# An encoder layer on one core: products queued behind the first score of their attention unit, and new places for the second half's buffers

## The chip, the cores and the metric

The kernel runs on one core of one Trainium2 chip. The metric is device microseconds of one execution, told as the median of several runs. The engines are named as the profile names them: PE (TensorE matmuls), PEld (its weight loads), DVE (VectorE), ACT (ScalarE), POOL (GpSimd) and SP (the queue from which nearly all DMAs are issued). SBUF is the on-chip memory, PSUM holds the results of matmuls, DRAM is the chip's large memory.

## What is computed

One layer of an encoder: windowed attention with grouped heads, then a SwiGLU feed-forward net (FFN), each between two norms and with shift, scale and gate from a modulation vector. Sequence 2048, width 1024, 16 query heads on 4 key heads of 64, FFN width 2816, all in float32. The reference, cut to what matters:

```python
mod = (c_act @ ada_w[i] + ada_b[i])[:, None, :]
sh1, sc1, g1, sh2, sc2, g2 = jnp.split(mod, 6, axis=-1)
h = rmsnorm(x, mix_norm_pre[i]) * (1.0 + sc1) + sh1
y = windowed_gqa_sink(h, att_w_qkv[j], att_w_o[j], att_sink[j], rel_bias)
x = x + g1 * rmsnorm(y, mix_norm_post[i])
h = rmsnorm(x, ffn_norm_pre[i]) * (1.0 + sc2) + sh2
y = swiglu(h, ffn_w_in[i], ffn_w_out[i])
x = x + g2 * rmsnorm(y, ffn_norm_post[i])
```

In `windowed_gqa_sink` every block of 128 queries sees three blocks of 128 keys, with a bias by distance and one more "sink" logit in the softmax.

## The kernel before

**Products.** Each float32 operand is split into a high part (ACT, L151) and the rest (DVE or POOL, L152), and a product of two 128-row blocks is three matmuls (`three`, L146 to L148). The tokens stand in four chunks of 512 columns. A "product" below means one such matmul of 512 columns.

**Stages.** First the queries, keys and values of chunks 0 and 1, and the first modulation rows (L238 to L366). Then attention: 64 units (`Unit`, L408), one for each block of 128 queries and key head. `scores` makes, for each of four heads, two score matmuls (L430), a DVE operation that adds the bias and finds the maximum (L435), and an exponential on ACT (L437); then POOL scales the rows by the reciprocal sum (L443). `values` runs LAG = 2 units later: three times four transposes on PE (L453), a split, and two value products (L458, L459); DVE puts the result together (L466). The scores have two PSUM banks (`psS`).

**Fillers.** While a unit waits for DVE, ACT and POOL, PE has other products to do. They come from generators: in the first 32 units the queries, keys and values of chunks 2 and 3 (`fillers_qkv`, L469: 24 tiles of 24 products), in the last 32 the output projections of chunks 0 to 2 (`fillers_o`, L593: again 24 tiles of 24). `Budget.pull` (L608) takes them out after each unit, 19 products per unit in the first half and 20 in the second (`FILL`, L47). The last six tiles of chunk 2 (`HOLD`, L54) are held until the last unit's first score. What is left after the last unit is drained (L667).

**What orders the work.** The program order is only a priority. A planner simulates the program's engines and queues and fixes, for each engine, the order of its instructions: at each moment the earliest instruction in program order that is ready by its reckoning. On the chip each engine then keeps that order and waits by semaphores. `tc.issue_after(ins)` adds an order: what is written inside on the engine of `ins` comes behind `ins` in that engine's queue. Each tile pool is a fixed stretch of SBUF from the left or the right; a tile of a new pool that lies over an old one waits until the old tiles there are no longer used. Tiles with the same tag share that tag's buffers.

**Around the projections.** `OProj.fill` (L521) loads the attention output (`ol`, four buffers), splits it, and makes eight tiles per chunk, each with its weight (`wo`). For chunk 0 the weight comes raw from `w_o` (one raw buffer), is split with POOL and stored in split form; chunks 1 and 2 load the split form (three buffers). After each tile it advances `ends` of the chunk before (L570): the norm's statistics, eight residuals (L502; three POOL operations each), statistics again, eight `make_h2` (L497), which store the FFN's input `h2_d`. Chunk 3 (`last_o`, L679) runs by itself after attention, and the ends of chunks 2 and 3 run as `late_residuals` (L837) beside the first FFN half, one step per block.

**Modulation rows.** `ada_load` and `ada_reduce` (L254, L259) make one of 48 rows of 128 numbers from a 512 KB weight and one DVE operation. Rows 0 to 24 are made before attention, rows 25 to 39 in units 1 to 31, two units between load and reduction, in the two raw buffers of the pool `ws`, which the fillers' raw weights share; rows 40 to 47 in units 34 to 50 (`ADA_UNITS`, L52).

**The FFN.** It uses a seven-product scheme for two by two blocks (`Block`, L739): each block of weights has four DVE sums, and each half of the sequence needs seven operands, some of them differences of `h2_d` blocks (`differences`, L701). For the first half these are made at the start: `h_blocks` (L877) loads blocks, two differences on DVE make the first two operands (L887, L888), then the blocks are loaded again for the rest. For the second half the differences are made within `late_residuals` and stored in `hd_d`, from which `Operands.load` (L731) gets them.

Of the kernel before, what the change touches and what calls it, by code (L numbers as in the profile page):

```python
# [11 lines left out]
F32 = mybir.dt.float32  # L12
# [33 lines left out]

FILL = (19, 20)  # L47
LAG = 2


ADA_A = 9
ADA_UNITS = (range(1, 32, 2), range(34, 52, 2))  # L52

# [18 lines left out]
def encoder_layer(ctx, tc, a):  # L72
# [4 lines left out]
    def open_pool(stack, name, bufs=1, side="left", space=None):  # L77
# [15 lines left out]
            for j in range(HT // 2)] for i in range(S // HALF)]  # L93
    hd_d = [{n: dram.tile([P, CH], F32, name=f"hd_d{j}_{n}") for n in OPERANDS if n[0] == "t"} for j in range(KT // 2)]
    h2_d = [dram.tile([P, KT, CH], F32, name=f"h2_d{c}") for c in range(NCH)]
# [142 lines left out]
    with ExitStack() as pa:  # L238
# [11 lines left out]
        sp.dma_start(cb_d, cb)  # L250
        cbs = [cb]
        tc.keep_in_program_order(act.preload_act_table_set("natural_log_exp_and_others"))
# [6 lines left out]
        def ada_reduce(t, w):  # L259
            dve.tensor_tensor_reduce(w, w, cbs[-1], 1.0, adab[:, t:t + 1], ALU.mult, ALU.add, mod[:, t:t + 1])  # L260

# [240 lines left out]
    def residual(c, k, y, xr, r, acc, alloc, eng=dve):  # L502
# [7 lines left out]
        else:  # L510
            sq = alloc(f"xsq{c}_{k}")
            act.activation(sq, y, AF.Square)
            pool.tensor_tensor(acc, acc, sq, ALU.add)

    class OProj:

# [4 lines left out]
        def fill(self, prev=None, hold=None):  # L521
# [11 lines left out]
            for n in range(KT):  # L533
                w = wop.tile([P, 2, KT, P], F32R, tag="w", name=f"wo{c}_{n}", bufs=2 if c == NCH - 1 else 3)
                if c in (0, NCH - 1):
                    raw = wop.tile([P, KT, P], F32, tag="raw", name=f"wor{c}_{n}", bufs=3 if c else 1)
                    sp.dma_start(raw, a["w_o"][n])
                    split(w[:, 0], w[:, 1], raw, dve if c else pool)
                    if c == 0:
                        sp.dma_start(wo_d[n], f(w))  # L540
                else:
                    sp.dma_start(f(w), wo_d[n])
                ps = psF.tile([P, CH], F32, tag="mm", name=f"py{c}_{n}")
                for k in range(KT):
# [77 lines left out]


    ada_units = [*ADA_UNITS[0], *ADA_UNITS[1]]
    HALF_ADA = len(ADA_UNITS[0]) - 1
    late = list(range(2 * KT + ADA_A, 6 * KT))
    units = [Unit(c, g, jb) for c in range(NCH) for g in range(KVH) for jb in range(JB)]
# [4 lines left out]
    oend = ExitStack()  # L632
    op = wop = yp = None
    for i, un in enumerate(units):
        if i == half:
            assert not waiting
# [17 lines left out]
        if i == 0:  # L654
            waiting = []
        if i in ada_units:
            for w in waiting:
                with tc.issue_after(un.red):
                    ada_reduce(*w)
            waiting = [ada_load(late.pop(0), ws if i < half else yp)] if i != ada_units[HALF_ADA] and late else []  # L660
# [7 lines left out]
    assert not late and not waiting  # L668
    dve.tensor_tensor(coef[:, 3, :], mod[:, 40:48], gains[:, 3, :], ALU.mult)
    att.close()  # L670
# [24 lines left out]
    def temp(name, tag="t", bufs=None):  # L695
        return tmp.tile([P, CH], F32, tag=tag, name=name, bufs=bufs)

    def temp0(name):
        return tmp0.tile([P, CH], F32, tag="t", name=name)

    def differences(b11, b12, b21, b22, give, engs=(pool, dve)):  # L701

        give("b11", b11)
        give("b21", b21)
        engs[0].tensor_tensor(b11, b12, b11, ALU.subtract)
        engs[1].tensor_tensor(b12, b22, b12, ALU.subtract)
        give("t3", b12)
        give("t1", b11)
        give("b22", b22)
        engs[0].tensor_tensor(b22, b22, b11, ALU.subtract)  # L710
        give("t2", b22)
        engs[1].tensor_tensor(b21, b21, b22, ALU.subtract)
        give("t4", b21)

    class Operands:
# [6 lines left out]
        def slot(self, n, k):  # L722
# [3 lines left out]
            return self.ops[n][k]  # L726

        def put(self, n, k, src):
            split(*self.slot(n, k), src, dve)

# [106 lines left out]
    def late_residuals():  # L837

        for c in range(CPH, NCH):
# [15 lines left out]
            for k in range(0, KT, 2):  # L855
# [6 lines left out]
                if c == NCH - 1:  # L862
                    first = [temp(f"ld{k + e}") for e in range(2)]
                    for e in range(2):
                        sp.dma_start(first[e], h2_d[c - 1][:, k + e, :])
                    differences(first[0], hs_[0], first[1], hs_[1],
                                lambda n, t: sp.dma_start(hd_d[k // 2][n], t) if n[0] == "t" else None)
                yield

    late = late_residuals()  # L870
    b21p = open_pool(early, "b21", K2)
    t3p = open_pool(early, "t3", K2)
    st0 = ExitStack()
    tmp0 = open_pool(st0, "tmp0", 10)
    half = Operands("0", K2, None)

    def h_blocks(k, names, st):  # L877
        b = []
        for n in names:
            b.append(temp0(f"fx{k}_{n}_{st}"))  # L880
            sp.dma_start(b[-1], h2_d[int(n[2]) - 1][:, 2 * k + (n[1] == "2"), :])
        return b

    with tc.high_priority(offset=1):
        for k in range(K2):
            b11, t1, t2 = h_blocks(k, ("b11", "b12", "b22"), 0)
            dve.tensor_tensor(t1, t1, b11, ALU.subtract)  # L887
            dve.tensor_tensor(t2, t2, t1, ALU.subtract)  # L888
# [9 lines left out]
    st0.close()  # L898
    tmp = open_pool(ffn, "tmp", 10, side="right")
    for hf in range(S // HALF):  # L900
        for t in range(HT - 2 if hf + 1 < S // HALF else HT - 1):
            hid = Hidden(half, t, hf)
            for i in range(7):
                hid.step(i)
            if hf == 0:
                next(late, None)
        if hf + 1 < S // HALF:
            pair = [Hidden(half, t, hf) for t in range(HT - 2, HT)]
            half = Operands("1", K2, lambda n, k: hd_d[k][n] if n[0] == "t" else
                            h2_d[CPH + int(n[2]) - 1][:, 2 * k + (n[1] == "2"), :])  # L910
            interleaved(pair, half)
    hid = Hidden(half, HT - 1, hf)
    for i in range(5):
# [231 lines left out]
```

## Time and profile before

| | us |
|---|---|
| median of 3 runs | 2191.41 |
| lowest to highest | 2188.45 to 2195.57 |
| the profiled execution | 2197.15 |
| its span in the trace | 2195.3 |
| first score of unit 0 | 181.3 |
| last product of the first half | 450.6 |
| first product of the projections | 482.2 |
| first score of unit 63, the last | 734.7 |

All times in the trace are microseconds from the span's start. A line of the timeline has the start, the duration, the engine (SPq: SP's queue), the line of the program, the operation, what it writes and reads, and in brackets the idle time before it with what ended it. A row of the stages has the stretch, its length, for each engine the busy time and the number of instructions, the clock that PE was granted (1.00 is full speed), the busy share of the DMA engines and GB/s; a row that is asked for a single line shows that line's instructions alone. Matmul records overlap, so the distance between two starts, not the duration, is what a matmul costs. A few records are missing from the trace.

### The profile page before, as it was taken

The page shows a single profiled execution, that of the slowest core. Times are in us where ns is not written, and L with a number is a line of the kernel's source. Part 1 is how long each engine was busy: PE and PEld are TensorE (multiplying, and loading weights), DVE is VectorE, ACT ScalarE, POOL GpSimd, SP SyncE. Part 2 cuts the span into 40 slices and gives each one's busy share as a digit, 9 for nine tenths or more (in the row PEclk, how much of TensorE's full clock was granted, in tenths as well). Part 3 has the DMA queues.
Part 4 walks back from the last instruction along what each step waited for, and adds up shares of the span by engine and source line. Part 5 has one row for each costly group of instructions (what it writes and reads, how often), then busy time and mean ns, then how long its engine had stood idle before and what let it go on. Part 6 is the DMA issues. An engine that isn't in the chain of part 4 may idle for free. (4 is left out here: it accounts for less than half of the span.)

```text
span 2195.3 us, 28935 instructions
## 1 busy us (share of the span) xinstructions
PE 2072.1 (94%) x9366; PEld 1677.9 (76%) x9366; DVE 1668.4 (76%) x2917; ACT 1080.6 (49%) x2125; POOL 774.2 (35%) x695
## 2 busy tenths in 40 slices
PE   6998999989989998899999989999999999998997
PEld 4786878767777776778888868888888788877886
DVE  8657676676766579877888797766664788999987
ACT  4546565677757664443434353333332654465432
POOL 3403333355696865434344522222221000220040
PEclk8998999999999999999999999999999999999998
DMA  8786665576865683444445663223231544348442
GB/s 287 252 272 225 189 195 166 167 232 213 301 222 204 202 311 129 152 163 153 161 156 180 220 226 110 107 101 115 101 105 41 205 149 148 127 152 278 158 130 101
DMA packets 195764, 390.05 MB, mean 178 GB/s; under 512 B 19563, under 2 KB 61596, under 8 KB 190492
## 3 DMA queue, kind: packets, MB, share of 16 engines
q1 hardware_dynamic: 195036, 387.68, 53.0%
q8 instruction: 74, 1.21, 0.2%
q14 instruction: 78, 0.64, 0.1%
q10 hardware_dynamic: 576, 0.52, 0.1%
HBM read 268.55 MB, written 119.57 MB: 177 GB/s over the span
## 5 line engine op out<-in xcount | busy, mean ns | idle before, releaser
L435 DVE CUSTOM_DVE_ANT_0 pr<-s,bias,nsink 128x384 f32<-128x384 f32 (+1 forms) x256 | 149.1, 595 | 121.6 <-PE s L430 100.0
L147 PE MATMUL pc_i<-ht,ws_i 128*128 128x512 f32 x528 | 207.2, 392 | 1.0 <-DVE ht L152 1.0
L146 PE MATMUL pc_i<-ht,ws_i 128*128 128x512 f32 x528 | 207.5, 393 | 0.6 <-DVE u_i L813 0.6
L148 PE MATMUL pc_i<-ht,ws_i 128*128 128x512 f32 x528 | 207.0, 392 | 0.0
L823 POOL TENSOR_TENSOR p_i<-p_i,u_i 128x512 f32<-128x512 f32 x44 | 80.0, 1818 | 326.8 <-DVE u_i L810 180.9
L437 ACT ACTIVATE pr<-pr,nm 128x385 f32<-128x385 f32 (+1 forms) x256 | 154.0, 605 | 72.3 <-DVE nm L435 64.2
L958 POOL TENSOR_TENSOR z<-z,z 128x512 f32<-128x512 f32 x32 | 53.8, 1696 | 358.6 <-DVE z L954 338.4
L443 POOL TENSOR_SCALAR pr<-pr,rs 128x384 f32<-128x384 f32 (+1 forms) x256 | 146.3, 591 | 92.4 <-DVE rs L441 90.5
L430 PE MATMUL s<-k,q 128*128 128x384 f32 (+1 forms) x512 | 138.9, 368 | 23.4 <-DVE nm L435 15.7
L151 ACT CAST ws_i<-s_i 128x512 fp32r<-128x512 f32 x132 | 81.5, 619 | 128.4 <-PE pc_i L148 122.3
L146 PE MATMUL pc_i<-hb,wa_i 128*128 128x512 f32 x352 | 139.3, 396 | 0.6 <-DVE b_i L807 0.6
L151 ACT CAST wa_i<-wiri 128x512 fp32r<-128x512 f32 x132 | 81.9, 620 | 117.2 <-PE pc_i L148 111.1
L148 PE MATMUL pc_i<-hb,wa_i 128*128 128x512 f32 x352 | 138.9, 395 | 0.0
L147 PE MATMUL pc_i<-hb,wa_i 128*128 128x512 f32 x352 | 138.8, 394 | 0.0
L152 DVE TENSOR_TENSOR plo<-t,phi 128x512 fp32r<-128x512 f32 x184 | 121.7, 683 | 13.2 <-ACT phi L151 12.3
L430 PEld LDWEIGHTS s<-k,q 128*128 128x128 f32 x512 | 89.7, 200 | 46.8 <-DVE nm L435 29.9
L146 PEld LDWEIGHTS pc_i<-ht,ws_i 128*128 128x128 f32 x528 | 99.3, 188 | 24.4 <-issue 1.0
L147 PEld LDWEIGHTS pc_i<-ht,ws_i 128*128 128x128 f32 x528 | 99.2, 188 | 23.7 <-DVE ht L152 1.5
L453 PE MATMUL t<-ident,pr 128*128 128x128 f32 x736 | 114.0, 281 | 2.5 <-DVE plo L152 2.3
L148 PEld LDWEIGHTS pc_i<-ht,ws_i 128*128 128x128 f32 x528 | 99.2, 188 | 22.2
L152 DVE TENSOR_TENSOR ws_i<-s_i,ws_i 128x512 fp32r<-128x512 f32 x132 | 107.7, 816 | 5.0 <-ACT ws_i L151 4.7
L152 DVE TENSOR_TENSOR wa_i<-wiri,wa_i 128x512 fp32r<-128x512 f32 x132 | 106.1, 804 | 5.6 <-ACT wa_i L151 5.3
(323 smaller groups left out, 6200.3 us busy)
## 6 DMA issues: line engine op xcount, KB each, us to landing
wiri<-w_in SPq DMA_DIRECT2D x88, 512.0 KB, 4.7
ada<-ada_w SPq DMA_DIRECT2D x48, 512.0 KB, 5.5
wiro<-w_out SPq DMA_DIRECT2D x48, 384.0 KB, 3.8
q_d<-e SPq DMA_DIRECT2D x64, 256.0 KB, 4.1
q<-q_d SPq DMA_DIRECT2D x16, 1024.0 KB, 5.5
wo<-wo_d SPq DMA_DIRECT2D x16, 1024.0 KB, 6.0
g_d_b<-p_i SPq DMA_DIRECT2D x44, 256.0 KB, 4.8
g_d_t<-p_i SPq DMA_DIRECT2D x40, 256.0 KB, 2.0
```

Of the source, the lines that this page charges most:

```text
L146: pe.matmul(ps, w[0], h[0], start=first, stop=False)
L147: pe.matmul(ps, w[0], h[1], start=False, stop=False)
L148: pe.matmul(ps, w[1], h[0], start=False, stop=last)
L151: act.copy(hi, src)
L152: return eng.tensor_tensor(lo, src, f(hi), ALU.subtract).ins
L430: m = pe.matmul(ps[:, :n], q[:, h, jb * P:(jb + 1) * P], kk[:, i, (jb + j0) * P:(jb + j1) * P], start=i == 0, stop=i == 1)
L435: red = dve.tensor_tensor_reduce(pr[:, h, :n], ps[:, :n], bias[g][:, h, j0 * P:j1 * P], -1.0, nsink[:, hh:hh + 1], ALU.add, ALU.min, nm[:, ...
L437: act.activation(pr[:, h, :n + 1], pr[:, h, :n + 1], AF.Exp, bias=nm[:, h:h + 1], scale=-1.0, accum_out=rs[:, h:h + 1])
L443: pool.tensor_scalar(pr[:, h, :n], pr[:, h, :n], rs[:, h:h + 1], 1.0, ALU.mult, ALU.mult)
L453: pe.transpose(pt[:, h * P:(h + 1) * P], pr[:, h, jj * P:(jj + 1) * P], ident)
L823: pool.tensor_tensor(sa, sa, b, ALU.mult)
L958: (pool if (i, x) in ((2, 2), (4, 4), (5, 5), (6, 6)) else dve).tensor_tensor(sums[hf, n2, x], sums[hf, n2, x], sums[hf, n2, y], ALU.add)
```

## The change

- **Products.** `FILL` becomes (18, 14), and `fill.pull` runs inside `tc.issue_after(un.first)`: on PE, whatever a pull writes stands behind the first score matmul of its unit. The final drain is outside.
- **Places.** The pools of the first half stand in another order (xs and nrm lowest, then hs and ev). The weight pool `ws` moves to the attention's own pools on the right and stays for both halves; the projection's weights use it too (`wop = ws`), with two buffers, and two raw ones for chunk 0. The pool of the o tiles, now six buffers, is opened lowest, where xs lay; 12 y buffers in place of 14. At the FFN's start `wi0` lies below `hA`.
- **Modulation.** Only rows up to 39 are made during attention. Rows 40 to 47 are made in the FFN (`late_ada`), each in two halves of 512 columns, one step per block after the late residuals; the second copy of the vector in the second half of attention is gone, and `coef[:, 3]` is made there.
- **The first FFN half's operands.** `OProj.ends` of chunk 1 makes the differences after each two `make_h2`, both engines' share on DVE, and stores the t operands in `hd_d[0]`; the FFN's start loads all operands from DRAM with `half.load`. `h_blocks`, `temp0` and `put` go. `ends` yields eight times in other places: after every fourth residual and every second `make_h2`.

```diff
-FILL = (19, 20)
+FILL = (18, 14)
...
-ADA_UNITS = (range(1, 32, 2), range(34, 52, 2))
+ADA_UNITS = range(1, 32, 2)
+
+OBUFS = 6
...
     com = ExitStack()
+    xs = open_pool(com, "xs", 8)
+    nrm = open_pool(com, "nrm")
     hs = open_pool(com, "hs", 2 * KT)
     ev = open_pool(com, "ev", 2)
-    nrm = open_pool(com, "nrm")
-    xs = open_pool(com, "xs", 8)
...
-    ws = open_pool(com, "ws", 2)
+    wop = ws = open_pool(att, "ws", 2, side="right")
...
-                t = op.tile([P, 2, 2, CH], F32R, tag="o", name=f"ol{c}_{g}", bufs=4)
+                t = op.tile([P, 2, 2, CH], F32R, tag="o", name=f"ol{c}_{g}", bufs=4 if c == NCH - 1 else OBUFS)
...
-                w = wop.tile([P, 2, KT, P], F32R, tag="w", name=f"wo{c}_{n}", bufs=2 if c == NCH - 1 else 3)
+                w = wop.tile([P, 2, KT, P], F32R, tag="w", name=f"wo{c}_{n}", bufs=2)
                 if c in (0, NCH - 1):
-                    raw = wop.tile([P, KT, P], F32, tag="raw", name=f"wor{c}_{n}", bufs=3 if c else 1)
+                    raw = wop.tile([P, KT, P], F32, tag="raw", name=f"wor{c}_{n}", bufs=3 if c else 2)
...
-                y = yp.tile([P, CH], F32, tag="y", name=f"y{c}_{n}", bufs=4 if c == NCH - 1 else 14)
+                y = yp.tile([P, CH], F32, tag="y", name=f"y{c}_{n}", bufs=4 if c == NCH - 1 else 12)
...
-                if k % 3 == 2:
+                if k % 4 == 3:
                     yield
-            yield
             r = self.stats("x", c)
             yield
             for k in range(KT):
                 make_h2(self.ys[k], c, k, r)
-                if k % 3 == 2:
+                if k % 2:
+                    if c == CPH - 1:
+                        first = [yp.tile([P, CH], F32, tag="xr", name=f"hf{j}", bufs=3) for j in (k - 1, k)]
+                        for j in range(2):
+                            sp.dma_start(first[j], h2_d[c - 1][:, k - 1 + j, :])
+                        differences(first[0], self.ys[k - 1], first[1], self.ys[k],
+                                    lambda n, t: sp.dma_start(hd_d[0][k // 2][n], t) if n[0] == "t" else None, (dve, dve))
                     yield
...
-    late = list(range(2 * KT + ADA_A, 6 * KT))
+    late = list(range(2 * KT + ADA_A, 5 * KT))
...
             com.close()
+            op = open_pool(oend, "op", OBUFS)
             yp = open_pool(oend, "yp")
-            cb = yp.tile([P, D], F32, tag="cb", name="cb2")
-            sp.dma_start(cb, cb_d)
-            cbs.append(cb)
-            wop = open_pool(oend, "wop", 2)
-            op = open_pool(oend, "op", 4)
             fill = Budget(fillers_o())
...
-        fill.pull(FILL[i >= half])
+
+        with tc.issue_after(un.first):
+            fill.pull(FILL[i >= half])
...
-    dve.tensor_tensor(coef[:, 3, :], mod[:, 40:48], gains[:, 3, :], ALU.mult)
     att.close()
...
+    wi = [open_pool(early, "wi0"), None]
     hA = open_pool(early, "hA", KT // 2)
-    wi = [open_pool(early, "wi0"), None]
...
+    def late_ada():
+
+        for i in range(2):
+            cols = slice(i * CH, (i + 1) * CH)
+            cb = temp(f"cb{i}", "r", 2)
+            sp.dma_start(cb, cb_d[:, cols])
+            for t in range(5 * KT, 6 * KT):
+                w = temp(f"ada{t}_{i}", "r", 2)
+                sp.dma_start(w, a["ada_w"][t][:, cols])
+                yield
+                dve.tensor_tensor_reduce(w, w, cb, 1.0, (mod if i else adab)[:, t:t + 1], ALU.mult, ALU.add, mod[:, t:t + 1])
+        dve.tensor_tensor(coef[:, 3, :], mod[:, 40:48], gains[:, 3, :], ALU.mult)
+
+    late = chain(late_residuals(), late_ada())
...
-    half = Operands("0", K2, None)
+    half = Operands("0", K2, lambda n, k: hd_d[0][k][n] if n[0] == "t" else
+                    h2_d[int(n[2]) - 1][:, 2 * k + (n[1] == "2"), :])
     with tc.high_priority(offset=1):
-        for k in range(K2):
-            b11, t1, t2 = h_blocks(k, ("b11", "b12", "b22"), 0)
-            dve.tensor_tensor(t1, t1, b11, ALU.subtract)
-            dve.tensor_tensor(t2, t2, t1, ALU.subtract)
-            half.put("b11", k, b11)
-            half.put("t2", k, t2)
+        half.load("b11", "t2")
...
     with tc.high_priority(offset=100):
-        for k in range(K2):
-            differences(*h_blocks(k, ("b11", "b12", "b21", "b22"), 1),
-                        lambda n, t: half.put(n, k, t) if n not in ("b11", "t2") else None)
+        half.load(*[n for n in OPERANDS if n not in ("b11", "t2")])
...
-            if hf == 0:
-                next(late, None)
+            next(late, None)
```

More of the change, by code (lines that the diff above doesn't have):

```diff
@@ L93, in encoder_layer @@
             for j in range(HT // 2)] for i in range(S // HALF)]
-    hd_d = [{n: dram.tile([P, CH], F32, name=f"hd_d{j}_{n}") for n in OPERANDS if n[0] == "t"} for j in range(KT // 2)]
+    hd_d = [[{n: dram.tile([P, CH], F32, name=f"hd_d{i}_{j}_{n}") for n in OPERANDS if n[0] == "t"}
+             for j in range(KT // 2)] for i in range(S // HALF)]
     h2_d = [dram.tile([P, KT, CH], F32, name=f"h2_d{c}") for c in range(NCH)]
@@ L250, in encoder_layer @@
         sp.dma_start(cb_d, cb)
-        cbs = [cb]
         tc.keep_in_program_order(act.preload_act_table_set("natural_log_exp_and_others"))
@@ L259, in ada_reduce @@
         def ada_reduce(t, w):
-            dve.tensor_tensor_reduce(w, w, cbs[-1], 1.0, adab[:, t:t + 1], ALU.mult, ALU.add, mod[:, t:t + 1])
+            dve.tensor_tensor_reduce(w, w, cb, 1.0, adab[:, t:t + 1], ALU.mult, ALU.add, mod[:, t:t + 1])
         wres = {}
@@ L513, in residual, with differences @@
             pool.tensor_tensor(acc, acc, sq, ALU.add)
+    def differences(b11, b12, b21, b22, give, engs=(pool, dve)):
+        give("b11", b11)
+        give("b21", b21)
+        engs[0].tensor_tensor(b11, b12, b11, ALU.subtract)
+        engs[1].tensor_tensor(b12, b22, b12, ALU.subtract)
+        give("t3", b12)
+        give("t1", b11)
+        give("b22", b22)
+        engs[0].tensor_tensor(b22, b22, b11, ALU.subtract)
+        give("t2", b22)
+        engs[1].tensor_tensor(b21, b21, b22, ALU.subtract)
+        give("t4", b21)
     class OProj:
@@ L621, in drain @@
             self.pull(1e9)
-    ada_units = [*ADA_UNITS[0], *ADA_UNITS[1]]
-    HALF_ADA = len(ADA_UNITS[0]) - 1
-    late = list(range(2 * KT + ADA_A, 6 * KT))
+    late = list(range(2 * KT + ADA_A, 5 * KT))
     units = [Unit(c, g, jb) for c in range(NCH) for g in range(KVH) for jb in range(JB)]
@@ L632, in encoder_layer @@
     oend = ExitStack()
-    op = wop = yp = None
+    op = yp = None
     for i, un in enumerate(units):
         if i == half:
-            assert not waiting
+            assert not waiting and not late
             fill.drain()
@@ L655, in encoder_layer @@
             waiting = []
-        if i in ada_units:
+        if i in ADA_UNITS:
             for w in waiting:
@@ L659, in encoder_layer @@
                     ada_reduce(*w)
-            waiting = [ada_load(late.pop(0), ws if i < half else yp)] if i != ada_units[HALF_ADA] and late else []
+            waiting = [ada_load(late.pop(0), ws)] if late else []
         if i >= LAG:
@@ L667, in encoder_layer @@
     fill.drain()
-    assert not late and not waiting
-    dve.tensor_tensor(coef[:, 3, :], mod[:, 40:48], gains[:, 3, :], ALU.mult)
     att.close()
@@ L696, in temp @@
         return tmp.tile([P, CH], F32, tag=tag, name=name, bufs=bufs)
[L698 to L713, printed above, removed]
     class Operands:
@@ L726, in slot @@
             return self.ops[n][k]
-        def put(self, n, k, src):
-            split(*self.slot(n, k), src, dve)
         def load(self, *names):
@@ L866, in late_residuals @@
                     differences(first[0], hs_[0], first[1], hs_[1],
-                                lambda n, t: sp.dma_start(hd_d[k // 2][n], t) if n[0] == "t" else None)
+                                lambda n, t: sp.dma_start(hd_d[1][k // 2][n], t) if n[0] == "t" else None)
                 yield
-    late = late_residuals()
+    def late_ada():
[10 more added lines that the diff above has]
+    late = chain(late_residuals(), late_ada())
     b21p = open_pool(early, "b21", K2)
     t3p = open_pool(early, "t3", K2)
-    st0 = ExitStack()
-    tmp0 = open_pool(st0, "tmp0", 10)
-    half = Operands("0", K2, None)
[L877 to L882, printed above, removed]
-    with tc.high_priority(offset=1):
-        for k in range(K2):
-            b11, t1, t2 = h_blocks(k, ("b11", "b12", "b22"), 0)
-            dve.tensor_tensor(t1, t1, b11, ALU.subtract)
-            dve.tensor_tensor(t2, t2, t1, ALU.subtract)
-            half.put("b11", k, b11)
-            half.put("t2", k, t2)
+    half = Operands("0", K2, lambda n, k: hd_d[0][k][n] if n[0] == "t" else
+                    h2_d[int(n[2]) - 1][:, 2 * k + (n[1] == "2"), :])
+    with tc.high_priority(offset=1):
+        half.load("b11", "t2")
     lasto.close()
@@ L894, in encoder_layer @@
     with tc.high_priority(offset=100):
-        for k in range(K2):
-            differences(*h_blocks(k, ("b11", "b12", "b21", "b22"), 1),
-                        lambda n, t: half.put(n, k, t) if n not in ("b11", "t2") else None)
-    st0.close()
+        half.load(*[n for n in OPERANDS if n not in ("b11", "t2")])
     tmp = open_pool(ffn, "tmp", 10, side="right")
@@ L904, in encoder_layer @@
                 hid.step(i)
-            if hf == 0:
-                next(late, None)
+            next(late, None)
         if hf + 1 < S // HALF:
             pair = [Hidden(half, t, hf) for t in range(HT - 2, HT)]
-            half = Operands("1", K2, lambda n, k: hd_d[k][n] if n[0] == "t" else
+            half = Operands("1", K2, lambda n, k: hd_d[1][k][n] if n[0] == "t" else
                             h2_d[CPH + int(n[2]) - 1][:, 2 * k + (n[1] == "2"), :])
             interleaved(pair, half)
+    assert next(late, None) is None
     hid = Hidden(half, HT - 1, hf)
```

## The prediction

> **What bounds the kernel now.** First the page's busy times:
>
> ```profile
> span 2195.3 us, 28935 instructions
> PE 2072.1 (94%) x9366; PEld 1677.9 (76%) x9366; DVE 1668.4 (76%) x2917; ACT 1080.6 (49%) x2125; POOL 774.2 (35%) x695
> ```
>
> TensorE (PE) is the bound, but its 94% is the busy share of pipelined records and hides slow stretches. So next the busy times by stage. I cut at the first score (181), the end of the first half of attention (461), the last unit's first score (735), the end of projection chunk 2 (786), the end of chunk 3 (840) and the first FFN blocks (900); the last row is a quiet FFN stretch.
>
> ```profile
> core 0: us, PE busy (x) PEld busy (x) DVE busy (x) ACT busy (x) POOL busy (x), PEclk, DMA share, GB/s
> 241.00:461.00 220.00, 212.62 (x1099) 175.09 (x1097) 149.49 (x386) 135.21 (x326) 80.63 (x126) 1.00 0.61 184
> 461.00:735.00 274.00, 249.21 (x1218) 199.00 (x1219) 188.47 (x466) 193.19 (x439) 197.58 (x228) 0.96 0.66 230
> 735.00:786.00 51.00, 46.90 (x220) 37.72 (x219) 27.10 (x45) 33.89 (x70) 38.34 (x38) 0.97 0.76 237
> 786.00:840.00 54.00, 51.84 (x226) 42.20 (x226) 45.90 (x52) 36.00 (x59) 36.86 (x15) 1.00 0.76 273
> 840.00:900.00 60.00, 47.26 (x183) 36.31 (x182) 54.68 (x75) 27.78 (x44) 28.13 (x13) 0.91 0.39 136
> 1330.00:1700.00 370.00, 370.00 (x1611) 302.02 (x1610) 244.18 (x353) 111.86 (x186) 84.32 (x56) 1.00 0.27 96
> ```
>
> The last row prices a product: 370 / 1611 = 0.230 us for 512 columns. By that price chunk 3 (226 x 0.230 = 52.0 of 54 us) is nearly full, and the FFN's start (183 x 0.230 = 42.0 of 60) loses 18 us. For attention I need the other matmuls, from the timeline on PE, by the distance from one start to the next:
>
> ```profile
> 219.03 0.85 PE L430 MATMUL s<-k,q 128*128 128x384 f32 x4
> 219.72 0.40 PE L147 MATMUL psq<-lo,ws 128*128 128x512 f32 x1
> ...
> 231.74 0.60 PE L453 MATMUL t<-ident,pr 128*128 128x128 f32 x4
> 232.09 0.60 PE L430 MATMUL s<-k,q 128*128 128x384 f32 x2
> ```
>
> Four scores take 0.69 us (0.172 each), four transposes 0.35 (0.087 each). A unit's own work is 8 scores, 12 transposes and 6 value products: 1.38 + 1.05 + 1.38 = 3.8 us. Then the counts by line and stage, products (L146 is every third one) first, scores second:
>
> ```profile
> 241.00:461.00 220.00, 61.50 (x153) 28.58 (x152) 1.00 0.61 184
> 461.00:735.00 274.00, 57.66 (x144) 27.23 (x145) 0.96 0.66 230
> ...
> 241.00:461.00 220.00, 51.19 (x198) 33.46 (x198) 1.00 0.61 184
> 461.00:735.00 274.00, 69.49 (x252) 43.67 (x252) 0.96 0.66 230
> ```
>
> First half: 459 products (105.6 us) and 198 / 8 = 24.75 units (94.1) fill 200 of 220 us; **20 us lost**. Second half: 432 products (99.4) and 31.5 units (119.7) fill 219 of 274; **55 us lost**. Those two and the FFN's start (18) are what a rearrangement can win.
>
> Why they are lost shows at single places. In the first half the raw weight slots are shared with the modulation rows:
>
> ```profile
> 303.60 0.34 SPq L256 DMA_DIRECT2D ada<-ada_w  x1
> 316.20 0.39 SPq L482 DMA_DIRECT2D wsr<-w_qkv  x1
> ...
> 314.88 1.28 DVE L260 CUSTOM_DVE_ANT_0 ada<-ada,cb,adab 128x1024 f32<-128x1024 f32 x1
> ...
> 413.89 0.50 PE L146 MATMUL psq<-hi,ws 128*128 128x512 f32 x1 [1.49 <-ACT ws L151]
> ```
>
> The weight load at 316.20 starts when the reduction at 314.88 has freed its slot. Products then come late and afterwards in a bunch. At the half the same happens once, larger:
>
> ```profile
> 465.69 0.34 SPq L537 DMA_DIRECT2D wor<-w_o  x1
> ...
> 479.88 1.04 ACT L151 CAST wo<-wor 128x1024 fp32r<-128x1024 f32 x1
> ...
> 483.45 2.38 POOL L152 TENSOR_TENSOR wo<-wor,wo 128x1024 fp32r<-128x1024 f32 x1
> ```
>
> The projection's first weight starts to load at 465.69, after the old pools closed, and is split at 483.45 + 2.38 = 486: from 461 to there attention runs almost without products. Later:
>
> ```profile
> 640.88 1.44 PE L430 MATMUL s<-k,q 128*128 128x384 f32 x4 [4.79 <-DVE nm L435]
> ...
> 632.97 7.33 DVE L669 TENSOR_TENSOR coef<-mod,gains 128x8 f32<-128x8 f32 x1
> ...
> L260 DVE CUSTOM_DVE_ANT_0 ada<-ada,cb,adab x8: 1280/1848/3514, 495.1 to 628.3; 128x1024 f32<-128x1024 f32 x8
> ...
> 640.00:660.00 20.00, 7.86 (x27) 5.07 (x27) 0.83 0.47 164
> 640.00:660.00 20.00, 0.00 (x0) 0.00 (x0) 0.83 0.47 164
> ...
> 640.00:650.00 10.00, 8.50 (x33) 6.67 (x33) 7.60 (x25) 9.04 (x24) 5.91 (x10) 0.66 0.60 206
> ```
>
> PE waits 4.79 us behind a tiny VectorE operation of 7.33 us, and the granted clock falls to 0.66. In 640 to 660 there are 27 scores (3.4 units) and no product at all: a bare unit takes 20 / 3.4 = 5.9 us for 3.8 us of PE work. With 20 products pulled per unit, the allowed ones are used up early and bare units follow.
>
> **The change, part by part.**
>
> *Products behind the first score, 18 and 14 per unit.* No product is added: 18 x 32 = 576 is just the first half's amount, and 14 x 32 = 448 leaves 128 of the second half's 576 for after the last unit, about the 144 that are held for it today. A unit then carries 3.8 + 18 x 0.230 = 7.9 us, later 3.8 + 14 x 0.230 = 7.0 us of PE work, both over the bare 5.9, so PE should bound every unit instead of some. In the first half the shared slots stay. A weight serves 48 products, and a modulation row comes in every second unit and leaves two units later. Written out, at 19 per unit six of the last ten weights are asked for in the very unit whose reduction frees their slot; at 18 it is four, and each a third of a unit into its products. 20 x 4/6 = 13 us remain, I take 12: **gain 8** (bounds 0 and 16).
>
> *Places and buffers, second half.* The weight pool outlives the half, so the raw projection weights can load before it; the o tiles lie where xs was, free early, with six buffers. That removes most of 461 to 486: 25 us that hold some 4 units, 25 - 4 x 3.8 = 10 us lost. Two weight buffers in place of three are enough at 24 / 14 x 7.0 = 12 us per weight; during the drain a weight lasts 24 x 0.230 = 5.5 us, and there a load can come late.
>
> *Modulation rows 40 to 47 and their coefficients go to the FFN.* VectorE loses 8 x 1.85 + 7.33 = 22 us here, of which PE felt 4.79 plus 10 x 0.34 = 3.4 of low clock: 8 us. There it gets 16 reductions of half the width, about 0.64 us each (half of 1.28), at most one per block with its load on SP, where VectorE works 244 of 370 us and the DMA share is 0.27: hidden, price 0; without that cover 16 x 0.64 = 10 us.
>
> *Bare units.* At 20 per unit the 576 - 144 = 432 products that aren't held last 21.6 units, so some ten of the 32 carry none; at 5.9 - 3.8 = 2.1 us that is 21 us. Together 10 + 8 + 21 = 39 of the 55 could go. What is late next is GpSimd (POOL): its 197.58 us would have to fit in 274 - 39 = 235, 84% busy, and it works in lumps:
>
> ```profile
> 607.18 10.06 POOL L505 TENSOR_TENSOR y<-y,no 128x512 f32<-128x512 f32 x8
> ```
>
> Ten microseconds in which no probabilities are scaled; the two units of lag (14 us) cover it, but not together with a split behind it. I take two thirds: **gain 25** (bounds 0 and 45).
>
> *Operand differences of the first FFN half, made in the projection's tail.* Before, blocks are loaded twice and subtracted at the FFN's start, and PE waits for the last of them:
>
> ```profile
> 849.36 0.79 PE L147 MATMUL pc_i<-ht,wa_i 128*128 128x512 f32 x1 [3.88 <-DVE ht L152]
> 884.97 0.80 PE L146 MATMUL pc_i<-hb,ws_i 128*128 128x512 f32 x1 [5.95 <-ACT p_i L794]
> ...
> 791.54 1.77 DVE L887 TENSOR_TENSOR fx_b<-fx_b,fx_b 128x512 f32<-128x512 f32 x1
> 798.81 0.69 DVE L888 TENSOR_TENSOR fx_b<-fx_b,fx_b 128x512 f32<-128x512 f32 x1
> ...
> 775.65 14.88 POOL L498 TENSOR_TENSOR y<-y,nx 128x512 f32<-128x512 f32 x8 [1.09 <-DVE nx L138]
> ...
> DMA to landing us min/median/max: 2.4/5.3/8.3
> ...
> L881 SPq DMA_DIRECT2D fx_b<-h_d x28: 319/323/1072, 779.6 to 844.7; - x28
> ```
>
> VectorE makes 16 differences as before (the other 8 were GpSimd's and vanish), but earlier, beside L498. Each costs 0.69 alone and 1.77 while L498 runs: 11 to 28 us, under the drain and chunk 3, where VectorE is idle for 24 of 51 and 8 of 54 us and sheds its 16 old ones. The round trip through DRAM adds two landings of 5.3 us, also under chunk 3. It adds 24 transfers of 0.26 MB, 6.3 MB; at 273 GB/s for a share of 0.76 that is 18 us of all engines, beside shares of 0.76, 0.76 and 0.39. On SP's queue they take 24 x 0.32 = 8 us, ahead of chunk 3's weights; the 28 loads that stood there stay as 28 operand loads. The wait of 3.88 and the smaller ones on the same splits should go; the 5.95 stays, since it is a table switch for the late statistics. Bounds -8 and 14, nearer the upper because the last operand is ready before the block: **gain 7**.
>
> The Trainium skill (SBUF — State Buffer, section Who interferes with whom) says that a VectorE operation with two SBUF inputs and a GpSimd one that reads SBUF exclude each other, the later one waiting in full. The 1.77 against 0.69 agrees; by it all 16 differences are slow and this part gives nothing, so the sum would be 33.
>
> **Sum:** 8 + 25 + 7 = 40 us. The profiled execution took 2197.15 us (1.85 outside its span), 5.7 above the median of 2191.4. It becomes 2157, the median **2151 us**.
>
> **The rivals.**
>
> *Only the places work (about 2171).* The products' order changes nothing because the real bound of a second-half unit is ScalarE and GpSimd (193 and 198 of 274 us). What remains is the half's 10, the modulation's 8, and little at the FFN: gain 20. For it: a static order from a planner need not fit the chip. Against it: stretches without any product exist and are long.
>
> *Products and chain add up (slower, about 2219).* A product may no longer run ahead of the next unit's score, and that score waits for VectorE. If products then stand behind scores and scores behind products, a unit takes the bare 5.9 plus 4.1 or 3.2 us: 32 x 10.0 + 32 x 9.1 + 128 x 0.230 = 640 us from 181 to 786 in place of 605: 35 slower, less 7 at the FFN. It decides from where more than 0.7 of the products lie outside the chain (280 / 32 = 8.75 per unit now, 8.75 - 5.9 = 2.85 of 4.1). Against it stands a stretch where both run together:
>
> ```profile
> 241.00:301.00 60.00, 11.06 (x49) 8.38 (x50) 1.00 0.62 201
> 241.00:301.00 60.00, 20.08 (x50) 9.21 (x49) 1.00 0.62 201
> ```
>
> 49 scores (6.1 units, 23.3 us) and 150 products (34.5) fill 57.8 of 60: over 20 products a unit, all of them under the chain.
> The Trainium skill (TensorE: Matmul & The Clock Gate, Step-by-step: what each phase is for) says that matmuls keep program order and only weight loads are pulled ahead. It speaks for this rival; the wait at 640.88 shows PE so standing.
>
> *Nothing moves (about 2191).* The planner had already spread the products so, and what the half wins the drain loses to two weight buffers.
>
> **How the numbers follow.** A measurement of this kernel tells 0.3%, some 6.6 us, from no change. Forecast (gain 24 to 70): 0.64. Only the places: 0.18. Nothing: 0.05. Slower: 0.08. A larger gain (all upper bounds, 16 + 45 + 14 = 75, 2116): 0.05. The range takes the forecast's span and the first rival, 2122 to 2182; the rest, under 0.2, is left out. Faster 0.64 + 0.18 + 0.05 = 0.87.
>
> **What would show it.** Right: products per unit near 18 and 14 with no unit between 461 and 735 without any; no 12 us without weights at the half; unit 63's first score near 700; no ada rows between 461 and 840; no wait on ht splits after chunk 3. Wrong: PE idle before scores on VectorE in most units (the second rival), or POOL over 90% busy and transposes waiting for scaled rows (the first). More than 70 us gained would mean that I took the lumps too seriously.

## The result, and the profile after

The changed kernel takes 2180.2 us (median of 4, 2178.68 to 2182.23), the kernel before beside it 2191.05: ratio 0.9949, 95% interval 0.993 to 0.9967. The change makes it 0.5% faster, 11 us. The forecast was 40 us, 2151.

The page of the changed kernel, on which TensorE is busy 94% as before, then its stages, cut where the last unit's first score now comes, 703, and in two stretches of the prediction:

```profile
span 2180.4 us, 29018 instructions
PE 2052.3 (94%) x9366; PEld 1667.5 (76%) x9366; DVE 1655.6 (76%) x2933; ACT 1076.8 (49%) x2125; POOL 740.7 (34%) x687
```

```profile
241.00:461.00 220.00, 214.98 (x1126) 179.40 (x1124) 154.52 (x402) 142.05 (x338) 88.48 (x133) 1.00 0.63 189
461.00:703.00 242.00, 233.61 (x1207) 192.66 (x1206) 162.85 (x437) 191.55 (x442) 178.05 (x217) 0.99 0.65 223
703.00:790.00 87.00, 51.72 (x206) 39.81 (x205) 40.91 (x53) 34.67 (x61) 52.32 (x46) 0.76 0.75 262
...
735.00:786.00 51.00, 26.97 (x86) 20.78 (x87) 27.64 (x23) 17.01 (x24) 22.10 (x14) 0.67 0.72 252
840.00:900.00 60.00, 58.02 (x250) 46.26 (x249) 56.10 (x80) 31.90 (x52) 16.92 (x12) 1.00 0.52 177
```

Unit 63 is told by its scores of 256 columns, those of the units just before it having 384:

```profile
702.80 0.40 PE L432 MATMUL s<-k,q 128*128 128x256 f32 x2
```

This first score comes at 702.8 us, 31.9 earlier than before. From there to 790, about where chunk 2 ends, TensorE is busy for 51.72 of 87 us; before, chunk 2 ended 51 us after that score, of which 46.90 were busy. The FFN's start is full: 250 matmuls in 840 to 900, 183 before. The chunk 3 product that ends last starts at 838.57 (before 837.57), so drain and chunk 3 gave back 32.9 us; the 168th FFN product comes at about 876.2 (before 889.8), so the start of the FFN won 14.6.

Inside the drain, TensorE's timeline shows two holes:

```profile
726.24 0.49 PE L461 MATMUL o<-plo,v 128*128 128x512 f32 x1
743.85 0.80 PE L131 MATMUL nstx<-nhix,ones 128*128 128x512 f32 x1 [17.11 <-DVE nhix L129]
744.44 0.63 PE L149 MATMUL py<-ol,wo 128*128 128x512 f32 x1
744.87 0.63 PE L150 MATMUL py<-ol,wo 128*128 128x512 f32 x1
...
749.36 0.40 PE L149 MATMUL py<-ol,wo 128*128 128x512 f32 x1
749.59 0.40 PE L150 MATMUL py<-ol,wo 128*128 128x512 f32 x1
...
754.41 0.50 PE L149 MATMUL py<-ol,wo 128*128 128x512 f32 x1 [1.86 <-ACT ysq L576]
...
755.91 0.60 PE L149 MATMUL py<-ol,wo 128*128 128x512 f32 x1
756.31 0.63 PE L150 MATMUL py<-ol,wo 128*128 128x512 f32 x1
...
761.42 0.40 PE L151 MATMUL py<-ol,wo 128*128 128x512 f32 x1
...
780.75 0.76 PE L149 MATMUL py<-ol,wo 128*128 128x512 f32 x1 [13.33 <-DMA wo<-wo_d]
```

**First hole, 17.11 us:** the statistics of chunk 1's residuals (`nstx`), with 19 products behind them in TensorE's queue that run as soon as it is past. Before, the wait there was 0.70:

```profile
763.26 0.50 PE L128 MATMUL nstx<-nhix,ones 128*128 128x512 f32 x1 [0.70 <-DVE nhix L126]
```

There 72 products lay between the last unit's first score and it; now 48 do, one tile less. What it waits for is on GpSimd:

```profile
698.26 10.07 POOL L507 TENSOR_TENSOR y<-y,no 128x512 f32<-128x512 f32 x8
708.29 1.29 POOL L508 TENSOR_TENSOR y<-y,xr 128x512 f32<-128x512 f32 x1
...
736.70 1.27 POOL L577 TENSOR_TENSOR yacc<-yacc,ysq 128x512 f32<-128x512 f32 x1 [3.40 <-ACT ysq L576]
737.92 4.45 POOL L515 TENSOR_TENSOR xacc<-xacc,xsq 128x512 f32<-128x512 f32 x2
```

The residuals begin at 698 and end at 742.4, 44 us in which scaling for the last units comes between them and GpSimd stands once for ScalarE, 3.40 us. **Second hole, 13.33 us:** a weight. SyncE's queue shows its load:

```profile
752.59 0.33 SPq L558 DMA_DIRECT2D wo<-wo_d  x1
...
759.92 0.32 SPq L611 DMA_DIRECT2D hd_d_t<-hf  x1
...
771.31 0.32 SPq L611 DMA_DIRECT2D hd_d_t<-y  x1
771.68 0.77 SPq L609 DMA_DIRECT2D hf<-h_d  x1
772.55 0.83 SPq L558 DMA_DIRECT2D wo<-wo_d  x1
```

The load of 772.55 stands behind stores of the early differences (L611) and of `h2` (L502), which wait for VectorE and ScalarE, as the waits of SyncE's queue from 752 to 790 say (total, times, longest; the first row is the load of 752.59, which waited for TensorE to come out of the first hole):

```profile
SPq L558 <- PE py L151: 8.7, 1, 8.7
SPq L611 <- DVE hf L521: 7.7, 4, 4.4
SPq L502 <- ACT y L501: 6.3, 2, 5.2
```

Its buffer's last reader is the 24th product from 754.41 on, at 761.42: the load leaves 11 us after that.

### The profile page after: what moved, and what is told of

Same layout as the page of the kernel before. It is cut to its first block, busy times and chain, and to the rows that moved or that the text cites. A ratio compares the mean times of both kernels' runs of the same rounds, so it can differ in the third digit from the quotient of the medians.

```text
span 2180.4 us, 29018 instructions
## 1 busy us (share of the span) xinstructions
PE 2052.3 (94%) x9366; PEld 1667.5 (76%) x9366; DVE 1655.6 (76%) x2933; ACT 1076.8 (49%) x2125; POOL 740.7 (34%) x687
## 5 line engine op out<-in xcount | busy, mean ns | idle before, releaser
L149 PE MATMUL pc_i<-ht,ws_i 128*128 128x512 f32 x528 | 207.6, 393 | 3.8 <-DVE b_i L801 1.5
L817 POOL TENSOR_TENSOR p_i<-p_i,u_i 128x512 f32<-128x512 f32 x44 | 71.5, 1625 | 304.9 <-DVE u_i L804 148.2
L432 PE MATMUL s<-k,q 128*128 128x384 f32 (+1 forms) x512 | 133.1, 359 | 15.3 <-DVE nm L437 8.4
L149 PE MATMUL pc_i<-hb,wa_i 128*128 128x512 f32 x352 | 138.9, 395 | 1.5 <-DVE u_i L791 1.4
L149 PEld LDWEIGHTS pc_i<-ht,ws_i 128*128 128x128 f32 x528 | 99.1, 188 | 28.2 <-DVE b_i L801 1.9
L149 PE MATMUL py<-ol,wo 128*128 128x512 f32 x256 | 104.9, 410 | 15.9 <-DMA wo<-wo_d 13.3
L154 ACT CAST phi<-t 128x512 fp32r<-128x512 f32 x184 | 101.9, 588 | 24.9 <-PE t L455 18.0
L432 PEld LDWEIGHTS s<-k,q 128*128 128x128 f32 x512 | 87.5, 194 | 32.8 <-DVE nm L437 17.3
```

The costliest lines, as they stand in the source:

```text
L149: pe.matmul(ps, w[0], h[0], start=first, stop=False)
L154: act.copy(hi, src)
L432: m = pe.matmul(ps[:, :n], q[:, h, jb * P:(jb + 1) * P], kk[:, i, (jb + j0) * P:(jb + j1) * P], start=i == 0, stop=i == 1)
L817: pool.tensor_tensor(sa, sa, b, ALU.mult)
```

## The experiments

"Gain" is (1 - ratio) x 2191 us. The four columns of times are from TensorE's timeline: unit 63's first score, the wait at chunk 1's second statistics, at a weight in the drain, and the longest at the FFN's first operand (a dash: under 1 us).

| run | median us | ratio (95%) | gain | score | statistics | weight | operand |
|---|---|---|---|---|---|---|---|
| the change | 2180.2 | 0.9949 (0.9930 to 0.9967) | 11 | 702.8 | 17.11 | 13.33 | - |
| e1 places only | 2174.3 | 0.9927 (0.9906 to 0.9949) | 16 | 720.6 | - | 6.48 | 2.00 |
| e2 products only | 2186.5 | 0.9977 (0.9964 to 0.9990) | 5 | 715.1 | 15.80 | - | - |
| e3 no queue rule | 2162.1 | 0.9864 (0.9844 to 0.9884) | 30 | 710.7 | - | 5.87 | 2.45 |
| e4 18 per unit | 2159.2 | 0.9856 (0.9836 to 0.9875) | 32 | 707.9 | - | 2.69 | 4.19 |
| e10 residuals on DVE | 2166.3 | 0.9898 (0.9882 to 0.9915) | 22 | 707.4 | 2.23 | 13.77 | - |
| e5 later statistics | 2157.8 | 0.9856 (0.9838 to 0.9873) | 32 | 698.4 | 10.62 | 1.30 | 3.19 |
| e6 third weight buffer | 2164.1 | 0.9886 (0.9868 to 0.9904) | 25 | 699.9 | 17.37 | - | - |
| e9 no early differences | 2181.4 | 0.9968 (0.9956 to 0.9981) | 7 | 700.1 | 16.71 | - | - |
| e7 stores on ACT's queue | 2168.6 | 0.9894 (0.9876 to 0.9913) | 23 | 701.1 | 16.91 | 1.32 | 1.56 |
| e16 e10 and e6 | 2154.9 | 0.9836 (0.9814 to 0.9857) | 36 | 701.8 | 2.85 | - | - |
| e20 e16 at 18 | 2158.7 | 0.9848 (0.9827 to 0.9869) | 33 | 712.1 | - | - | 11.22 |
| e22 e10 and e5 at 18 | 2160.0 | 0.9863 (0.9839 to 0.9886) | 30 | 707.1 | - | - | 15.83 |
| e23 e16, no queue rule | 2167.4 | 0.9900 (0.9881 to 0.9920) | 22 | 712.3 | - | - | 11.69 |
| e24 e16 and e7 | 2158.2 | 0.9857 (0.9836 to 0.9878) | 31 | 701.0 | 2.85 | - | - |
| e25 e5, e7 and e10 | 2154.1 | 0.9844 (0.9825 to 0.9864) | 34 | 699.1 | - | - | 13.83 |

**e1 and e2: the two halves of the change.** e1 is the changed kernel, e2 the kernel before, with

```diff
# e1, from the changed kernel
-FILL = (18, 14)
+FILL = (19, 20)
-        with tc.issue_after(un.first):
-            fill.pull(FILL[i >= half])
+        fill.pull(FILL[i >= half])
# e2, from the kernel before
-FILL = (19, 20)
+FILL = (18, 14)
-        fill.pull(FILL[i >= half])
+        with tc.issue_after(un.first):
+            fill.pull(FILL[i >= half])
```

> The changed kernel with the budgets 19 and 20 of before and without the rule that queues the products behind the first score: the places, buffers, early differences and late modulation alone. Theory A (the queue moved the last score 27 us forward and the drain gave that back, 17 us at the second statistics and 13 us at a late weight): the places keep what they bring at the half boundary (10 us) and at the start of the FFN (10 us), the last unit's first score stays near 725, the drain stays near 50 us: 2165 to 2175, at or below the changed kernel. Theory B (the places bring all of the 10.9 us and the queue nothing): 2180. Theory C (the queue brings it all): 2191.

> The kernel before with the budgets 18 and 14 and the products queued behind the first score, and its own places, buffers, modulation rows and differences. Theory A: attention ends some 15 us earlier and the drain pays it back, as in the changed kernel, with three weight buffers but the second statistics one tile later: 2183 to 2193. Theory B (queue worth nothing): 2191. Theory C (the queue brings the gain): 2180.

The 27 us of e1's expectation count from the unit's third score, at 707.93; from its first they are 32. The places alone gain 16 us, by their estimate more than the whole change (the intervals overlap). The products alone bring the last score 20 us forward and gain 5: the wait of 15.80 us at the statistics is there in the old places too, with three weight buffers and the statistics a tile later. So the first hole belongs to the products, and the second doesn't come from them alone.

**e3 and e4: rule and budget.** e3 drops only the `issue_after`, e4 only sets `FILL = (18, 18)`.

> The changed kernel, budgets 18 and 14 kept, without the rule that puts the products behind the first score. It prices the queue rule by itself. Theory A: the units of the second half are gone through nearly as fast, since the budget is what shortens them, and the drain is as long: 2178 to 2186. Theory B: the same as the changed kernel within 0.3% as well. Theory C (the rule is what keeps scores from standing behind products): attention ends 15 to 25 us later and the run takes 2195 to 2205.

> The changed kernel with 18 products per unit in the second half in place of 14, queued the same way. Theory A (what is left for the drain is what is lost there): about 120 products of 0.230 us, 28 us of TensorE work, go from the drain into units that idle; chunk 1's end begins some four units earlier, its residuals lie under attention and the 17 us at the second statistics shrink to under 5: 2160 to 2172. Theory D (units are bound by TensorE, so that each product put back lengthens its unit by the 0.230 us that it saves in the drain): 2178 to 2183.

For e3 all three expectations missed: without the rule the kernel is 19 us faster than with it. By 690 us e3 and e4 have both done all 432 products that aren't held, the changed kernel 408. Chunk 1's first statistics come at 673 in place of 690, its residuals lie under attention, and the hole is gone; in e4 they come at 673 too. Nothing says yet whether the rule costs anything by itself.

**e10 and e5: the first hole.**

```diff
# e10
-                         self.acc, rot(yp, "nsq", 4), pool)
+                         self.acc, rot(yp, "nsq", 4), dve if c else pool)
# e5: ends yields as before, 14 buffers for y
-                if k % 4 == 3:
+                if k % 3 == 2:
                     yield
+            yield
             r = self.stats("x", c)
...
+                if k in (1, 3):
                     yield
```

> The changed kernel with the residual additions of chunk 1 on VectorE in place of GpSimd (16 of GpSimd's 24 operations of the residuals remain). TensorE's order is nearly that of the changed kernel. Theory A1 (TensorE stands 17.11 us at chunk 1's second statistics because GpSimd's residuals are late, with products behind it that could run): GpSimd's part of the residuals, 29.3 us by eight multiplications, eight additions and seven sums of squares, loses its eight additions of 1.2 us, the wait falls to between 6 and 9, and the run to 2168 to 2174. Rival A2 (the wait covers a weight load or the SP queue that is late anyway, and the 13.33 us at the weight grows by what this one loses): 2178 to 2183.

> The changed kernel with the end of a chunk given out as before: second statistics one product tile later, 14 buffers for y in place of 12. Theory A1: 24 more products of 0.230 us stand ahead of the statistics, so the wait of 17.11 us falls by 5.5 and the run to 2172 to 2176. Rival A2 (GpSimd sets the end, whatever stands in TensorE's queue): 2179 to 2183.

TensorE's two holes in e10:

```profile
734.39 0.80 PE L131 MATMUL nstx<-nhix,ones 128*128 128x512 f32 x1 [2.23 <-DVE nhix L129]
...
772.61 0.77 PE L149 MATMUL py<-ol,wo 128*128 128x512 f32 x1 [13.77 <-DMA wo<-wo_d]
```

With the first hole down by 14.9 us and the second as it was, the run gains 11 us on the changed kernel: the wait was on the path. In e5 the statistics still wait, but 6.5 us less, about what the 5.5 us of products put ahead of them are worth. It gained 20 where I expected 4 to 8, because the second hole went too: the weight's load was now placed ahead of the stores, at 747.67 (the first of the differences' stores leaves at 755.63).

**e6, e9 and e7: the second hole.** e9 is the changed kernel with the first half's operands made at the FFN's start, by the code of before.

```diff
# e6
+            wx = open_pool(att, "wx", 1, side="right")
             fill = Budget(fillers_o())
...
-                w = wop.tile([P, 2, KT, P], F32R, tag="w", name=f"wo{c}_{n}", bufs=2)
+                third = c < NCH - 1 and (KT * c + n) % 3 == 2
+                w = (wx if third else wop).tile([P, 2, KT, P], F32R, tag="w", name=f"wo{c}_{n}", bufs=1 if third else 2)
# e7
-                                    lambda n, t: sp.dma_start(hd_d[0][k // 2][n], t) if n[0] == "t" else None, (dve, dve))
+                                    lambda n, t: act.dma_start(hd_d[0][k // 2][n], t) if n[0] == "t" else None, (dve, dve))
```

> The changed kernel with a third buffer for the output projection's weights in the second half of the attention (every third tile in a pool of its own). Theory A3 (the 13.33 us at the weight come from having two buffers: the load waits until TensorE has read the tile before last): the load is issued a tile earlier, the wait goes to under 3 us: 2167 to 2172. Rival A4 (the load stands in SyncE's queue behind stores of differences that wait for VectorE, or its transfer is slow for the traffic): the third buffer leaves most of the wait: 2177 to 2182.

> The changed kernel without the differences of the first half made in the drain; they are made at the start of the FFN as in the kernel before. Theory A4 (their loads, stores and VectorE work in the drain delay the weights by 13.33 us): the wait at the weight goes, the waits for split operands at the start of the FFN come back (10 to 16 us): 2178 to 2186, with the drain 10 us shorter and the start of the FFN 10 to 16 us longer. Theory A3 (two weight buffers): the drain as in the changed kernel, the start longer: 2188 to 2196.

> The changed kernel with the stores of the drain's differences issued from ScalarE's queue in place of SyncE's; two weight buffers and all traffic as they were. Theory A4 (the last weight's load was issued at 772.55 us, though its buffer's reader had ended some 10 us before, because it stands in SyncE's queue behind stores that wait for the differences): the load goes out as its buffer falls free, the wait of 13.33 us falls to under 4 and the run to 2165 to 2171. Theory A3 (two buffers are too few, or the traffic is too dense, whatever the queue): 2177 to 2183.

SyncE's queue in e7, and then in e6:

```profile
750.19 0.33 SPq L558 DMA_DIRECT2D wo<-wo_d  x1
759.92 0.38 SPq L558 DMA_DIRECT2D wo<-wo_d  x1
763.86 0.32 SPq L609 DMA_DIRECT2D hf<-h_d  x1
```

```profile
750.30 0.33 SPq L559 DMA_DIRECT2D wo<-wo_d  x1
757.62 0.32 SPq L612 DMA_DIRECT2D hd_d_t<-hf  x1
```

In e7 the program differs only in the queue of 16 stores, and the same load leaves at 759.92 in place of 772.55, when its buffer falls free; the wait shrinks to 1.32. Two buffers and the traffic were enough: the load stood in a queue. The third buffer mends it from the other side, because its last load needn't wait and is placed before the stores. Without the differences (e9) the hole is gone as well, but what they won is lost behind it, in smaller waits from 783 on and at the FFN's start: 139 matmuls in 860 to 900 against 172 in e7. From e9 to e7, 16 us, is what the early differences are worth once their stores stand elsewhere.

```profile
873.32 0.80 PE L149 MATMUL pc_i<-hb,ws_i 128*128 128x512 f32 x1 [5.89 <-ACT p_i L788]
```

This row of e9 is the wait of 5.95 us of before; in the changed kernel no wait above 1 us is left from 840 to 900.

**e16 and e20: both mends.**

> The changed kernel with both mends that shortened it alone: chunk 1's residual additions on VectorE, which took 13.9 us off, and the third weight buffer, which took 16.1 off. Theory A (two separate waits on the way to the end): the gains add, 2180.2 less 30.0, so 2147 to 2155. Rival (the two waits cover one another, or a third thing stands behind them): 2160 to 2166, the better of the two or little under it.

> Both mends with 18 products per unit in place of 14. Theory A (18 per unit gained 21 us only by keeping the two waits of the drain small): with the waits mended the budget matters little, within 5 us of the run with both mends at 14. Rival theory E (14 also starves TensorE elsewhere: the drain of one engine's work after attention is longer than it need be): 8 us or more below the run at 14.

By the ratios e10 gains 11.2 us on the changed kernel, e6 13.8, both together 24.8: they add. 2154.9 is where the forecast had put the change, 2151. At 18 per unit the score comes 10 us later and a third wait stands behind chunk 3, at the FFN's first operand. Of e16 and e20:

```profile
730.66 0.79 PE L131 MATMUL nstx<-nhix,ones 128*128 128x512 f32 x1 [2.85 <-DVE nhix L129]
```

```profile
818.09 0.79 PE L149 MATMUL pc_i<-hb,wa_i 128*128 128x512 f32 x1 [11.22 <-ACT hb L154]
```

**e22, e24 and e25: combinations.** e22 is e10 and e5 at `FILL = (18, 18)`, e24 is e16 with e7's queue, e25 is e5, e7 and e10 at (18, 14).

> 18 products per unit, residual additions on VectorE, second statistics one tile later with 14 buffers for y, and two weight buffers. Theory A: the wait at the statistics is under 2 us whichever of the three brings it, so they do not add: 2152 to 2158. Rival (each brings its own part): 2145 or less.

> Both mends, and the differences' stores from ScalarE's queue as well. Theory A4 (the third weight buffer already takes the load ahead of those stores, so nothing of that wait is left): 2152 to 2157, the same as with both mends. Rival (weights or the FFN's first loads still stand behind the stores): 2145 to 2150.

> 14 products per unit with the queue rule, residual additions on VectorE, second statistics one tile later (14 buffers for y), the differences' stores from ScalarE's queue, two weight buffers. Theory A (all known waits of the drain mended, 2.9 us left at the statistics gone as well): 2150 to 2155. Rival (the start of the FFN now waits for its first operand, as it did with 18 per unit): 2156 to 2162.

None differs from e16 by more than the intervals tell: mended in one way, the holes give nothing a second time. In e22 and e25, as in e20, the FFN's first operand becomes late instead (15.83 and 13.83 us); what makes it late stays open. In e25 this is the rival's wait, though the time lies in the range of Theory A. e16 and e25, at 2155 and 2154, are the fastest here, 34 to 36 us below the kernel before. Some expectations whose theory held missed the time: e4, e10 and e6 came out 1 to 3 us faster than their ranges and e5 14, e22, e24 and e23 (below) 1 to 2 us slower.

**e23: the rule by itself.** e16 without the `issue_after`.

> Both mends (residual additions on VectorE, third weight buffer), 14 products per unit, without the rule that queues the products behind the first score. Theory A (the rule speeds up the attention and costs only by the two waits that it sets off): with these mended the rule's run is the faster one, so 2158 to 2166 here against 2155 with the rule. Theory F (the rule costs time by itself, in the attention too): 2140 to 2150.

With the holes mended the run with the rule is 14 us faster (ratios 0.9836 and 0.9900); while they were open the rule cost 19. The score comes 10.5 us earlier with it (701.8 against 712.3), but these are not the 14 us: the drain gives them back, and the last product of chunk 3 starts at 807.62 with the rule and at 807.05 without. The difference comes after that. In e23 TensorE then waits for the FFN's first operand, while in e16 the first FFN product runs among the last ones of chunk 3. Of e23 and e16:

```profile
807.05 0.39 PE L151 MATMUL py<-ol,wo 128*128 128x512 f32 x1
819.12 0.80 PE L149 MATMUL pc_i<-hb,wa_i 128*128 128x512 f32 x1 [11.69 <-ACT hb L154]
```

```profile
802.58 0.39 PE L149 MATMUL pc_i<-hb,wa_i 128*128 128x512 f32 x1
```

e20, e22 and e25 have the rule and wait for the same operand, so the missing rule isn't what makes it late in general, and what the rule is worth by itself stays open. Against e3, the fastest run without the rule, e16 is 6 us faster, and the intervals overlap.

## Why the prediction was right or wrong

**Direction and attention: right.** By lines, products (L149 is every third) and then scores (L432) of the changed kernel:

```profile
241.00:461.00 220.00, 61.31 (x152) 28.57 (x152) 1.00 0.63 189
461.00:703.00 242.00, 57.81 (x144) 27.41 (x145) 0.99 0.65 223
```

```profile
241.00:461.00 220.00, 52.86 (x208) 35.01 (x207) 1.00 0.63 189
461.00:703.00 242.00, 62.99 (x244) 40.23 (x242) 0.99 0.65 223
```

First half: 456 x 0.230 + 26 x 3.8 = 203.7 of 220, so 16 us are lost where 20 were: 4 gained, 8 forecast. Second half, up to the last unit's first score: 432 x 0.230 + 30.5 x 3.8 = 215.3 of 242: 27 lost where 55 were, 28 gained, 25 forecast. Projections begin at 461.99 (before 482.20). Unit 63 starts 31.9 us earlier, 33 forecast.

**Start of the FFN: more than forecast,** 14.6 for 7. The waits on `ht` went as said; the 5.95 us, which I had kept as a table switch of the late statistics, went with them, though the switch is still there (two table loads of 1.28 us on ScalarE, at 862.07 and 864.07). VectorE's differences did slow down beside GpSimd, as this pair of rows of the changed kernel shows (with `make_h2`'s GpSimd part running, and after it):

```profile
767.87 1.75 DVE L522 TENSOR_TENSOR y<-y,y 128x512 f32<-128x512 f32 x1
...
776.57 0.69 DVE L522 TENSOR_TENSOR y<-y,y 128x512 f32<-128x512 f32 x1
```

The rule of the Trainium skill (SBUF — State Buffer, section Who interferes with whom), that a VectorE operation with two SBUF inputs and a GpSimd one that reads SBUF exclude each other, agrees with the durations while both engines run: eight of the sixteen differences took 1.27 to 1.78 us, seven 0.69. The prediction's reading of it, that all sixteen are slow and the part gives nothing, does not agree, since the part is worth 16 us (e9 to e7).

**The drain: wrong, and this is the step that failed.** The forecast said that 14 per unit "leaves 128 of the second half's 576 for after the last unit, about the 144 that are held for it today", and so took the drain as unchanged, at no cost. The count of products was the same, 144 in both kernels; their company was not. With 14 per unit and the rule chunk 1's end starts 13 us before the last unit's first score (690.05 to 702.80; before 33, 702.04 to 734.7), so the residuals run into the drain, and the statistics, moved one tile forward, stand in TensorE's order ahead of products that could have covered part of it: 17.11 us. The tile accounts for some 6.5 of them (e5); with the statistics in their old place e2 still waits 15.80. The differences' stores, costed as "8 us, ahead of chunk 3's weights", stand ahead of chunk 2's, and wait for VectorE there: 13.33 us. I had written that "there a load can come late" and blamed two buffers, with no price; e7 shows that the queue was to blame. Together the holes are 30.4 us, the forecast missed by 29, and the two mends bring it to within 4. That closeness is partly luck: in e16 the start of the FFN wins 13.5 us where 7 were forecast, and drain and chunk 3 still lose 3.

**The rivals.** "Nothing moves" had 0.05 and came nearest to what happened: attention gained and the drain paid, though through the queues. "Only the places work" came near in price (20 forecast, 16 in e1) but not in cause, for the products did move. "Products and chain add up" did not come about: in e16 the rule shortens attention (701.8 against 712.3 in e23).

## What to carry to other kernels

When work is moved from under a long phase to its end, the count of what is left says nothing: list, for each engine's queue, what now stands ahead of what, and who feeds the head. A matmul of statistics, or a store of a late result on the queue that carries the weights, stopped everything behind it here. A change that costs time (here the rule, 19 us) should be judged again once the waits that it uncovers are mended: then the run with it was the faster one, though by a third wait that, of the two, only the run without it had.

## What the runs showed of the hardware

After the hole of 17.11 us the products run 0.43 us apart (744.44 to 744.87) in place of 0.23 (749.36 to 749.59), until about 748.7: ten products, 2 us more than the hole itself. The Trainium skill (TensorE: Matmul & The Clock Gate, section What's actually happening) says that TensorE starts at half rate after idling until it has been busy for some 3.4 us; the trace agrees in kind, with 4.9 us from 743.85. After a pause of only 1.86 us, though (to 754.41), six products run at full rate and then eight 0.43 us apart, from 755.91 to 759.30; e7, e6, e9 and e16 show the same slow stretch, of about 3 us, after their pause of 1.85 or 1.86 us; e2, after one of 1.87 us, does not. So the half rate came without a long hole too, and what brings it these runs don't settle.
